# HGRN2's output gate by seven block products with weight sums made by DMA, in turn with a branch gate

## The chip, the cores and the metric

The kernel runs on one core of one Trainium2 chip. The metric is the device time of one execution in microseconds (us), as the median of several. The engines are named as in the profile: PE is TensorE (PEld its weight load), DVE is VectorE, ACT is ScalarE, POOL is GpSimd, and SP is SyncE, which here only issues DMAs.

## The reference

One decoder block on 256 tokens of width 1024 in fp32. Two token mixers read the same x by one input projection, are merged by gates, and a SwiGLU FFN follows.

```python
proj = einsum('bsd,dn->bsn', x, w_in)
hq, hf, hi, hg, mq, mk, mv, gates = split(proj)     # each 1024 wide, gates 2048
y = hgrn2_mixer(hq, hf, hi, lb)                     # the recurrence, 8 heads of 128
y = rms_norm(y, hgrn_norm_w) * silu(hg)             # norm per head; hg is the output gate
za = y @ w_branch_a                                 # branch a
zb = moba_attention(mq, mk, mv) @ w_branch_b        # branch b
ga, gb = split(sigmoid(gates + b_gate))             # the branch gates
x = layer_norm(ALPHA * x + (ga * za + gb * zb) @ w_out)
x = layer_norm(ALPHA * x + swiglu_ffn(x))
```

The step at issue is `hg = x @ w_in[:, 3072:4096]`, a product of 256x1024 by 1024x1024, and `silu(hg)`. Beside it are `gb`, a product of the same size, and the recurrence, whose work is done between the products.

## The kernel before

**Products.** TensorE multiplies numbers of a shorter format, so every fp32 operand is split into a high and a low half, and each product is made of three matmuls: high by high, low by high and high by low (`feat_steps`, lines 277 to 279; token-major in L296 to L298). x comes once, transposed, as xTr with its halves xTh and xTl. The weights come in tiles of 1 MB (128x2048 fp32), in the order of the list that `plan` makes. `stage` loads tile i into `raw` from SP's queue (pool `wraw`, three buffers), ACT casts it to the high half (`wh`, L195), DVE subtracts to get the low half (`wl`, L197); `wh` and `wl` have four buffers each, and `fetch` keeps the split three tiles ahead of TensorE (LOOKAHEAD = 3). A feature-major stage (hg, gb, ga, hq: `feat_pair`) takes four tiles of 256 columns with 48 matmuls of 128x256 each; a token-major one (hi: `tok_chunk`) has 128x512 matmuls.

**The order of the first 160 us** is that of the text: hf, hq, hi (tiles 8 to 11), hg (tiles 12 to 15), gb (16 to 19), ga (20 to 23), then the attention's mk, mq and mv. A scheduler then sets each engine's own row of instructions. Each engine works its row off in order, so an instruction that waits holds up all behind it.

**The recurrence** (`hgrn_steps`) is a generator that other stages advance by `side.step()`. It first makes Qt = Qg·Fg and kq = Kt·Qg with its halves kqh and kql, the diagonal products sd0 to sd3 on PE (L388, L389) and their masked copies into SD on DVE (L390). Then come seven levels (sc0 to sc6): two groups of matmuls (L404), masked copies into SD, and updates of Qt, Kt and Tt on DVE (L406 to L417). Then the state product sc7, the outputs o with their norm `on` (L445), and the transposes ot, in which `ya = pt * hgs` is split for branch a.

**The output gate**, before, is feature-major: Sigmoid on ACT, and DVE's `hgs = hg * norm weight * sigmoid(hg)` (L489). One level follows each hg, gb and ga tile.

**Banks.** PSUM has two pools of four banks: `mm` for the projections, `aux` for the recurrence. A product can begin when a bank of its pool has been read out; hi's four banks are freed by ACT's copies into hv (L481).

**The FFN's last part** (`quad`, q0 to q6) already uses seven products in place of eight for a 2x2 block product; the sums of its weight blocks are made by DVE (`mix`, table MIXES).

Of the kernel before, what the change touches and what calls it, by code (L numbers as in the profile page):

```python
# [10 lines left out]
F32 = mybir.dt.float32  # L11
# [6 lines left out]
P = 128  # L18
# [19 lines left out]
MIXES = (((0, 4, 0), 1, None), ((0, 4, 512), 0, 1), ((4, 4, 512), 0, 2), (None, 1, 2),  # L38
         (None, 2, None), ((4, 4, 0), 0, 3), (None, 3, None))
# [33 lines left out]
def plan():  # L73

    tiles = []

    def add(w, k0, kn, c0, n, held=False):
        tiles.append((w, k0, kn, c0 if isinstance(c0, tuple) else (c0,), n, held))
# [12 lines left out]
    feat("w_in", 0, 1024)  # L91
    tok("w_in", 2048, 1024)
    feat("w_in", 3072, 1024)
    feat("w_in", 8192, 1024)
    feat("w_in", 7168, 1024)
    for c in range(2):
        feat("w_in", 5120 + c * 512, 512)
        feat("w_in", 4096 + c * 512, 512)
        tok("w_in", 6144 + c * 512, 512)
    feat("w_branch_a", 0, 1024)  # L100
    feat("w_branch_b", 0, 1024)
    for k in range(0, KC, 2):
# [20 lines left out]
def hybrid_layer_kernel(ctx: ExitStack, tc, x, xT, vecs, wts, ln1_w, ln1_b, ln2_w, ln2_b, consts, out):  # L123
# [55 lines left out]
    def stage(pieces=None, eng=nc.vector):  # L179
        i = state["next"]  # L180
        if i >= len(loads):
            return
        state["next"] += 1
        _, _, k, _, _, held = loads[i]
        src = source(i).rearrange("p (k c) -> p k c", k=k)
        view = lambda z: z.rearrange("p (k c) -> p k c", k=k)
        raw = view(wraw.tile([P, 2048], F32, tag="raw", name=f"raw{i}"))
        if held:
            h, l = view(slot(f"wh{i}", F32R)), view(slot(f"wl{i}", F32R))
        else:  # L190
            h = view(whi.tile([P, 2048], F32R, tag="h", name=f"wh{i}"))
            l = view(wlo.tile([P, 2048], F32R, tag="l", name=f"wl{i}"))
        for ks in ks_of(pieces or (k,)):
            nc.sync.dma_start(raw[:, ks, :], src[:, ks, :])
            nc.scalar.copy(h[:, ks, :], raw[:, ks, :])  # L195
            yield
            eng.tensor_sub(l[:, ks, :], raw[:, ks, :], r32(h[:, ks, :]))  # L197
            yield
        ready.append((h, l))

    raws = []

    def mix():


        i = state["next"]
        state["next"] += 1
        tile, into, other = loads[i][-1]
        if tile is not None:
            kept = dict(pool=late, tag="late") if len(raws) < 2 else dict(pool=wraw, tag="raw")  # L210
            raws.append(kept.pop("pool").tile([P, 2048], F32, name=f"raw{i}", **kept))
            nc.sync.dma_start(raws[-1], source(i))
        into = len(raws) - 1 if tile is not None and other is None else into
        if other is not None:
            nc.vector.tensor_add(raws[into], raws[into], raws[other])  # L215
        h = whi.tile([P, 2048], F32R, tag="h", name=f"wh{i}")
        l = wlo.tile([P, 2048], F32R, tag="l", name=f"wl{i}")
        split(h, l, raws[into])
        view = lambda z: z.rearrange("p (k c) -> p k c", k=KW // 2)
        ready.append((view(h), view(l)))  # L220

    def fetch(ahead=LOOKAHEAD):
        while state["next"] < len(loads) and len(ready) < 1 + ahead:
            if isinstance(loads[state["next"]][-1], tuple):
                mix()
            else:
                list(stage())
        return ready.pop(0)
# [36 lines left out]
    def feat_pair(name, ah=None, al=None):  # L265
        ah, al = (xTh, xTl) if ah is None else (ah, al)
        wh, wl = fetch()
        ps = mm.tile([P, 2, T], F32, tag="mm", name=name)
        for f in range(2):
            feat_steps(ps[:, f, :], wh, wl, f, ah, al, range(KC))  # L270
        return ps

    def feat_steps(ps, wh, wl, f, ah, al, ks, k0=0):
        wcol = slice(f * P, (f + 1) * P)
        for k in ks:
# [3 lines left out]
            nc.tensor.matmul(ps, wl[:, k, wcol], ah[:, kk, :], start=False, stop=(kk == KC - 1))  # L279

# [68 lines left out]
    for j in range(4):  # L349
# [3 lines left out]
        for f in range(2):  # L353
            h = 2 * j + f
            nc.vector.scalar_tensor_tensor(Qg[:, :, h, :], by_half(ps[:, f, :]), lb[:, H + h:H + h + 1],
                                           by_half(sg[:, f, :]), op0=ALU.mult, op1=ALU.mult)
# [18 lines left out]
    def hgrn_steps():  # L375
        Qt, SD = halves(slot("Qt")), halves(slot("SD"))
        Tt = slot("Tt")
        nc.vector.tensor_mul(Qt, Qg, Fg)
# [13 lines left out]
        yield  # L392
        tot, size = Fg, NT * H * P
# [34 lines left out]
        on = slot("on").rearrange("p (t d) -> p t d", t=NT)  # L428
        for g in range(2):
            for u in range(NT):  # L430
# [14 lines left out]
                nc.vector.tensor_tensor(dst, ps, st[:, 8:12, None].to_broadcast([P, 4, P]), op=ALU.mult)  # L445
            yield
            for j in range(2):
# [27 lines left out]

    side = Steps()
# [3 lines left out]
    for c in range(2):  # L480
        for _ in tok_chunk(f"hi{c}", lambda t, ps: nc.scalar.copy(hv[:, t, c * 512:(c + 1) * 512], ps)):  # L481
            side.step()
    for j in range(4):
        ps = feat_pair(f"hg{j}")
        sg = hd2.tile([P, 2, T], F32, tag="sg", name=f"sgg{j}")
        nc.scalar.activation(sg, ps, AF.Sigmoid)
        for f in range(2):
            h = 2 * j + f
            nc.vector.scalar_tensor_tensor(hgs[:, h, :], ps[:, f, :], nw[:, h:h + 1], sg[:, f, :],  # L489
                                           op0=ALU.mult, op1=ALU.mult)  # L490
# [3 lines left out]
    def gates(name, b0):
        g = slot(name).rearrange("p (c t) -> p c t", c=KC)
        for j in range(4):
            ps = feat_pair(f"{name}{j}")
            for f in range(2):
                c = 2 * j + f
                nc.scalar.activation(g[:, c, :], ps[:, f, :], AF.Sigmoid, bias=bg[:, b0 + c:b0 + c + 1])  # L500
            side.step()
        return g
# [277 lines left out]
    def quad_product(n):  # L780
# [7 lines left out]
        for k in range(KW // 2):  # L788
            nc.tensor.matmul(ps, lh[:, k, :], wh[:, k, :], start=(k == 0), stop=False)
            nc.tensor.matmul(ps, lh[:, k, :], wl[:, k, :], start=False, stop=False)  # L790
            nc.tensor.matmul(ps, ll[:, k, :], wh[:, k, :], start=False, stop=(k == KW // 2 - 1))
# [19 lines left out]
    for j in range(EARLY, NF, 2):  # L811
        n = j // 2 % 2
        sums = []
        if j == KW:
            mixing = mixed_a()
        for i, (nm, p, tag) in enumerate([("g", mm, "mm"), ("u", aux, "aux")]):
# [8 lines left out]
            if j == KW:  # L825
                sh, sl = next(mixing)
# [59 lines left out]
```

## Time and profile before

| | |
|---|---|
| median of 3 runs | 508.87 us (508.49 to 509.5) |
| the profiled execution | 508.92 us, its span 506.9 us |
| mean granted TensorE clock | 0.995 of full |
| weight tiles | 78 DMAs of 1 MB by SP, median 4.8 us from issue to landing |
| bytes moved | 91.68 MB, of which 3.15 MB by POOL's queue (q0) |
| hi, hg, gb, ga (53.7 to 160 us) | PE busy 106.30 us of 106.30, DVE 89.25, ACT 51.13, POOL 4.02 |

Times in the rows of the profile are us from the span's start. A row of the timeline has the start, the duration, the engine, the line in the kernel, the operation, its output and inputs by the program's names, and in brackets how long the engine had been idle and what it waited for. A row of a group has, behind the bar, the busy time, the mean time of one in ns, and the idle time ahead of the group.

### The profile page before, as it was taken

Reading aid. Unit: us, or ns where it says so; the run is one execution under the profiler, and the core shown is the slowest. Engines: PE = TensorE matmul, PEld = TensorE weight load, DVE = VectorE, ACT = ScalarE, POOL = GpSimd, SP = SyncE. Lnnn points to the kernel's source line nnn. Section 1 sums busy time; section 2 is a strip of 40 time slices with the busy share of each in tenths; the row PEclk is TensorE's granted clock in tenths of the full one; section 3 lists DMA queues with packets and bytes.
Section 4 is the critical chain, followed back from the end, with each engine's and each line's share of the span. In section 5 each row is a group of like instructions: output and inputs, shape, how many; then the busy total and the mean of one; then the engine's idle time right before and its main releaser. Section 6 shows DMA issues by size and latency. Waiting matters only on the chain.

```text
span 506.9 us, 7897 instructions
## 1 busy us (share of the span) xinstructions
PE 496.7 (98%) x3308; PEld 457.9 (90%) x3308; DVE 363.8 (72%) x409; ACT 257.8 (51%) x312; POOL 39.9 (8%) x33
## 2 busy tenths in 40 slices
PE   8999999999999999999999999999999999999994
PEld 7999889999999998998999988888888888888884
DVE  4777799997565454676665599655687566989656
ACT  5795354354355554566544463354656655574500
POOL 0000000000020064263000000000000000000001
PEclk9999999999999999999999999999999999999998
DMA  7978444244423544544645776346545544154402
GB/s 236 393 280 319 180 170 164 93 162 162 166 85 140 194 167 173 182 163 149 250 180 185 277 272 210 123 166 215 200 167 180 220 181 166 36 213 178 154 1 83
DMA packets 15714, 91.68 MB, mean 181 GB/s; under 512 B 1856, under 2 KB 3008, under 8 KB 5696
## 3 DMA queue, kind: packets, MB, share of 16 engines
q1 hardware_dynamic: 14832, 88.04, 48.3%
q0 software_dynamic: 848, 3.15, 1.8%
q8 instruction: 26, 0.43, 0.3%
q14 instruction: 8, 0.07, 0.0%
HBM read 90.13 MB, written 1.05 MB: 180 GB/s over the span
## 4 chain that ended last, share of the span: by engine, by line
PE 94%; DMA 4%; DVE 1%; ACT 0%; SPq 0%; issue 0%; DVEq 0%
PE fu L748 7%; PE fg L748 7%; DMA raw<-in_wts_dram 4%; PE fg L749 3%; PE fu L749 3%; PE sc L404 3%; PE wd L612 3%; PE wd L610 3%; PE wd L611 3%; PE mk L279 2%; PE hq L279 2%; PE hq L278 2%; PE hq L277 2%; PE mk L278 2%; PE zb L279 2%; PE za L279 2%
## 5 line engine op out<-in xcount | busy, mean ns | idle before, releaser
L197 DVE TENSOR_TENSOR wl<-raw,wh 128x2048 fp32r<-128x2048 f32 (+2 forms) x84 | 177.4, 2114 | 92.5 <-ACT wh L195 92.2
L195 ACT CAST wh<-raw 128x2048 fp32r<-128x2048 f32 (+2 forms) x84 | 148.3, 1768 | 129.9 <-issue 14.1
L748 PE MATMUL fg<-x1p,wh 128*128 128x512 f32 x144 | 50.5, 394 | 0.0
L748 PE MATMUL fu<-x1p,wh 128*128 128x512 f32 x144 | 50.4, 394 | 0.0
L749 PE MATMUL fg<-x1p,wl 128*128 128x256 f32 x144 | 40.0, 278 | 0.0
L749 PE MATMUL fu<-x1p,wl 128*128 128x256 f32 x144 | 39.9, 277 | 0.0
L748 PEld LDWEIGHTS fu<-x1p,wh 128*128 128x128 f32 x144 | 27.0, 187 | 6.2
L748 PEld LDWEIGHTS fg<-x1p,wh 128*128 128x128 f32 x144 | 27.0, 187 | 6.1
L749 PEld LDWEIGHTS fg<-x1p,wl 128*128 128x128 f32 x144 | 27.0, 188 | 0.1
L749 PEld LDWEIGHTS fu<-x1p,wl 128*128 128x128 f32 x144 | 27.0, 188 | 0.0
L611 PE MATMUL wd<-wl,ah 128*128 128x512 f32 (+1 forms) x70 | 24.1, 347 | 0.0
L612 PE MATMUL wd<-wh,al 128*128 128x512 f32 (+1 forms) x70 | 24.1, 347 | 0.0
L610 PE MATMUL wd<-wh,ah 128*128 128x512 f32 (+1 forms) x70 | 23.7, 346 | 0.0
L279 PE MATMUL hf<-xTh,wl 128*128 128x256 f32 x64 | 18.6, 291 | 1.0 <-DVE wl L197 1.0
L277 PE MATMUL hf<-xTh,wh 128*128 128x256 f32 x64 | 18.2, 284 | 1.0 <-ACT wh L195 1.0
L279 PE MATMUL za<-yah,wl 128*128 128x256 f32 x64 | 18.5, 288 | 0.0
L278 PE MATMUL za<-yal,wh 128*128 128x256 f32 x64 | 18.4, 288 | 0.0
L277 PE MATMUL hg<-xTh,wh 128*128 128x256 f32 x64 | 18.4, 288 | 0.0
L172 ACT CAST wh<-raw 128x2048 fp32r<-128x2048 f32 x7 | 13.4, 1912 | 9.7 <-DVE raw L215 3.8
L173 DVE TENSOR_TENSOR wl<-raw,wh 128x2048 fp32r<-128x2048 f32 x7 | 16.0, 2287 | 3.2 <-ACT wh L172 3.2
L277 PE MATMUL mk<-xTh,wh 128*128 128x256 f32 x64 | 18.3, 286 | 0.0
L278 PE MATMUL mq<-xTl,wh 128*128 128x256 f32 x64 | 18.3, 286 | 0.0
(249 smaller groups left out, 1447.1 us busy)
## 6 DMA issues: line engine op xcount, KB each, us to landing
raw<-in_wts_dram SPq DMA_DIRECT2D x78, 1024.0 KB, 4.8
raw<-in_wts_dram SPq DMA_DIRECT2D x8, 256.0 KB, 5.0
xTr<-in_xT_dram SPq DMA_DIRECT2D x8, 128.0 KB, 4.9
raw<-in_wts_dram SPq DMA_DIRECT2D x2, 512.0 KB, 6.1
xr<-in_x_dram POOLq DMA_DIRECT2D x1, 1024.0 KB, 5.4
wb<-in_ln_w_dram POOLq DMA_DIRECT2D x2, 512.0 KB, 5.3
wb<-in_ln_b_dram POOLq DMA_DIRECT2D x2, 512.0 KB, 6.2
out_dram<-x SPq DMA_DIRECT2D x4, 256.0 KB, 2.0
```

What stands on the lines that cost most here:

```text
L173: nc.vector.tensor_sub(dst_l, src, r32(dst_h))
L195: nc.scalar.copy(h[:, ks, :], raw[:, ks, :])
L197: eng.tensor_sub(l[:, ks, :], raw[:, ks, :], r32(h[:, ks, :]))
L277: nc.tensor.matmul(ps, wh[:, k, wcol], ah[:, kk, :], start=(kk == 0), stop=False)
L278: nc.tensor.matmul(ps, wh[:, k, wcol], al[:, kk, :], start=False, stop=False)
L279: nc.tensor.matmul(ps, wl[:, k, wcol], ah[:, kk, :], start=False, stop=(kk == KC - 1))
L404: nc.tensor.matmul(ps[:, a, :], KL[:, h, :], later(Qt, n, h, 1), start=True, stop=True)
L610: nc.tensor.matmul(ps, lh(kk)[:, ts], wh[:, k, ns], start=(kk == base), stop=False)
L611: nc.tensor.matmul(ps, lh(kk)[:, ts], wl[:, k, ns], start=False, stop=False)
L612: nc.tensor.matmul(ps, ll(kk)[:, ts], wh[:, k, ns], start=False, stop=(kk == ktot - 1))
L748: nc.tensor.matmul(ps, wh[:, k, wcol], x1p.both(k), start=(k == 0), stop=False)
L749: nc.tensor.matmul(ps[:, 0, :], wl[:, k, wcol], x1p[0, k, slice(0, T)], start=False, stop=(k == KC - 1))
```

## The change

The output gate becomes token-major, and its product is made of seven block products (`quad_stage`, `block_product`) of 12 matmuls of 128x512 each, in place of 192 matmuls of 128x256. The tokens are two blocks of 128, the inputs two of 512, the columns two of 512. Four of the products multiply sums of weight blocks (s and t, three states of s) by differences of activations (`differences`: xs, with halves xSh and xSl, made during hq).

The sums are made in the `raw` buffers: four blocks are loaded by SP as before, and then POOL issues DMAs that add a block from DRAM onto a buffer (`accum_op`). The table BY_DMA has, for each product, the buffer that it uses and what is done ahead of it: s = block 11; s += block 12; t = block 12 and t += block 22; s += 22; v = 21; u = 22; s += 21. Every state of s is split (ACT, DVE) before the next sum may overwrite it.

```diff
+BY_DMA = (("s", (("load", "s", 11),)), ("s", (("onto", "s", 12),)), ("t", (("load", "t", 12), ("onto", "t", 22))),
+          ("s", (("onto", "s", 22),)), ("v", (("load", "v", 21),)), ("u", (("load", "u", 22),)),
+          ("s", (("onto", "s", 21),)))
+GATES_BEHIND = (0, 2, 4, 5)
...
-    feat("w_in", 3072, 1024)
-    feat("w_in", 8192, 1024)
+    for n, recipe in enumerate(BY_DMA):
+        mix("hg", "w_in", 0, 3072, recipe)
+        if n in GATES_BEHIND:
+            feat("w_in", 8192 + 256 * GATES_BEHIND.index(n), 256)
...
+            if op == "load":
+                own, tag = (late, "late") if name == "wd" and dst in "st" else (wraw, "raw")
+                raws[key] = own.tile([P, 2048], F32, tag=tag, name=f"raw{i}{dst}")
+                nc.sync.dma_start(raws[key], wts[src])
+            elif op == "onto":
+                nc.gpsimd.dma_start(raws[key], wts[src], accum_op=ALU.add)
...
+    def block_product(ps, lh, ll, wh, wl, first=True, last=True):
+        for k in range(KW // 2):
+            go = dict(skip_group_check=not (first and last))
+            nc.tensor.matmul(ps, lh[:, k, :], wh[:, k, :], start=first and k == 0, stop=False, **go)
+            nc.tensor.matmul(ps, lh[:, k, :], wl[:, k, :], start=False, stop=False, **go)
+            nc.tensor.matmul(ps, ll[:, k, :], wh[:, k, :], start=False, stop=k == KW // 2 - 1, **go)
...
+        if j == 0:
+            xs = slot("xs")[:, 0:1024].rearrange("p (i k t) -> p i k t", i=2, k=KW // 2)
+            xSh, xSl = mixed4(slot("xSh", F32R)), mixed4(slot("xSl", F32R))
+            mixing = differences(lambda t, k: xTr[:, k:k + 4, t * P:(t + 1) * P], xs, xSh, xSl)
+        if j in (1, 2):
+            next(mixing)
...
-        kq, kqh, kql = slot("kq"), slot("kqh", F32R), slot("kql", F32R)
+        kq, kqh, kql = flat(Qg), slot("kqh", F32R), slot("kql", F32R)
...
+                row = on[:, u, g * 512:(g + 1) * 512]
+                nc.vector.tensor_mul(row, row, hgs[:, u, g * 512:(g + 1) * 512])
...
-                ya = hd2.tile([P, 2, T], F32, tag="sg", name=f"ya{g}{j}")
-                nc.vector.tensor_mul(ya, pt, hgs[:, h0:h0 + 2, :])
-                split(yah[:, h0:h0 + 2, :], yal[:, h0:h0 + 2, :], ya)
+                for a in range(2):
+                    h = h0 + a
+                    nc.scalar.activation(yah[0][:, h, :], pt[:, a, :], AF.Copy, scale=nw[:, h:h + 1])
+                    nc.vector.scalar_tensor_tensor(yal[0][:, h, :], pt[:, a, :], nw[:, h:h + 1], r32(yah[0][:, h, :]),
+                                                   op0=ALU.mult, op1=ALU.subtract)
...
-        sg = hd2.tile([P, 2, T], F32, tag="sg", name=f"sgg{j}")
-        nc.scalar.activation(sg, ps, AF.Sigmoid)
-        for f in range(2):
-            h = 2 * j + f
-            nc.vector.scalar_tensor_tensor(hgs[:, h, :], ps[:, f, :], nw[:, h:h + 1], sg[:, f, :],
-                                           op0=ALU.mult, op1=ALU.mult)
-        side.step()
...
-    gb = gates("gb", KC)
-    ga = gates("ga", 0)
+    def gate_pair(g, name, b0, j, p=mm):
+        ps = feat_pair(f"{name}{j}", p=p)
+        for f in range(2):
+            c = 2 * j + f
+            nc.scalar.activation(g[:, c, :], ps[:, f, :], AF.Sigmoid, bias=bg[:, b0 + c:b0 + c + 1])
+    gb = slot("gb").rearrange("p (c t) -> p c t", c=KC)
+    hg = quad_stage("hg", xTh, xTl, xSh, xSl, hgs, lambda z, src: nc.scalar.activation(z, src, AF.Silu))
+    for j in range(4):
+        next(hg)
+        gate_pair(gb, "gb", KC, j, aux)
+        if j >= 1:
+            side.step()
+    list(hg)
+    ga = slot("ga").rearrange("p (c t) -> p c t", c=KC)
+    for j in range(4):
+        gate_pair(ga, "ga", 0, j)
+        side.step(2)
```

`quad_stage` makes the products in the banks b[0] to b[3] of `mm`, and combines them with one ACT copy each of b[0] and b[2], six DVE sums or differences of 128x512, and ACT's Silu. The FFN's `quad` does the same work as before by the shared functions. The tiles are now numbered 12 (s), 13 (gb0), 14 (s), 15 (t), 16 (gb1), 17 (s), 18 (v), 19 (gb2), 20 (u), 21 (gb3), 22 (s), and 23 to 26 for ga. The gates gb are written into banks of `aux`.

The first place is VectorE's row at the end of hi and the beginning of hg. Names have the tile's number: wl12 is the low half of tile 12, raw12s the buffer of s. Before:

```order
L378 TENSOR_TENSOR Qt_677<-Qg_96,Fg_94 128x2048
L381 TENSOR_TENSOR kq_681<-Kt_95,Qg_96 128x2048
L197 TENSOR_TENSOR wl12_754<-raw12_752,wh12_753 128x2048
L414 TENSOR_TENSOR Kt_95<-Kt_95,Fg_94 128x512x2
L383 TENSOR_TENSOR kql_683<-kq_681,kqh_682 128x2048
L197 TENSOR_TENSOR wl13_805<-raw13_803,wh13_804 128x2048
L197 TENSOR_TENSOR wl14_852<-raw14_850,wh14_851 128x2048
L390 TENSOR_TENSOR SD_678<-sd0_687,ident_89 128x512
```

And now the same place:

```order
L419 TENSOR_TENSOR Qt_685<-Qg_96,Fg_94 128x2048
L188 TENSOR_TENSOR wl12_744<-raw12s_741,wh12_743 128x2048
L422 TENSOR_TENSOR Qg_96<-Kt_95,Qg_96 128x2048
L212 TENSOR_TENSOR wl13_777<-raw13_775,wh13_776 128x2048
L456 TENSOR_TENSOR Kt_95<-Kt_95,Fg_94 128x512x2
L424 TENSOR_TENSOR kql_689<-Qg_96,kqh_688 128x2048
L188 TENSOR_TENSOR wl14_807<-raw12s_741,wh14_806 128x2048
L431 TENSOR_TENSOR SD_686<-sd0_693,ident_89 128x512
```

In both, the low half of tile 14 stands ahead of SD's product with sd0; tile 14 was a plain load, and is now the second state of s, in the buffer that tile 12 was split from.

The second place is TensorE's row at the end of hi. Before:

```order
L296 MATMUL hi1_1_802<-wh11_706,xTh_86 128x512
L389 MATMUL sd0_687<-kql_683,ones_91 128x512
L389 MATMUL sd1_691<-kql_683,ones_91 128x512
L389 MATMUL sd2_695<-kql_683,ones_91 128x512
L389 MATMUL sd3_699<-kql_683,ones_91 128x512
L297 MATMUL hi1_1_802<-wh11_706,xTl_87 128x512
```

Eleven more matmuls of hi follow there, and then hg0. Now:

```order
L337 MATMUL hi1_1_774<-wl11_713,xTh_86 128x512
L430 MATMUL sd0_693<-kql_689,ones_91 128x512
L430 MATMUL sd1_697<-kql_689,ones_91 128x512
L430 MATMUL sd2_701<-kql_689,ones_91 128x512
L430 MATMUL sd3_705<-kql_689,ones_91 128x512
L295 MATMUL gb0_869<-xTh_86,wh13_776 128x256
```

The sd products now stand behind all of hi, and gate gb0, which takes its bank from the same pool as sd0 to sd3, follows them directly; hg0 stands 29 matmuls later.

The third place is the row of POOL's queue, which had no DMA between the program's start and the attention. Now:

```order
L941 UNCONDITIONAL_BRANCH
L231 DMA raw15t_843<-in_wts_dram 128x2048
L231 DMA raw12s_741<-in_wts_dram 128x2048 x3
L487 ISA
L487 TENSOR_TENSOR ost00_1522<-ost00_1522,half_92 128x4
```

The accumulate onto t stands first, ahead of the three onto s.

More of the change, by code (lines that the diff above doesn't have):

```diff
@@ L37 @@
 KW = 8
-MIXES = (((0, 4, 0), 1, None), ((0, 4, 512), 0, 1), ((4, 4, 512), 0, 2), (None, 1, 2),
-         (None, 2, None), ((4, 4, 0), 0, 3), (None, 3, None))
+BY_SUMS = (("s", (("load", "s", 11),)), ("s", (("load", "t", 12), ("sum", "s", "t"))),
+           ("s", (("load", "u", 22), ("sum", "s", "u"))), ("t", (("sum", "t", "u"),)), ("u", ()),
+           ("s", (("load", "v", 21), ("sum", "s", "v"))), ("v", ()))
+BY_DMA = (("s", (("load", "s", 11),)), ("s", (("onto", "s", 12),)), ("t", (("load", "t", 12), ("onto", "t", 22))),
+          ("s", (("onto", "s", 22),)), ("v", (("load", "v", 21),)), ("u", (("load", "u", 22),)),
+          ("s", (("onto", "s", 21),)))
+GATES_BEHIND = (0, 2, 4, 5)
 ORDER_DOWN = (0, 1, "t", 2, "t", 3, "t", 4, "t", 5, 6) + ("t",) * HOLD_DOWN
@@ L73, in plan, with block, mix @@
 def plan():
-    tiles = []
-    def add(w, k0, kn, c0, n, held=False):
-        tiles.append((w, k0, kn, c0 if isinstance(c0, tuple) else (c0,), n, held))
+    blocks, steps = [], []
+    def block(*key):
+        if key not in blocks:
+            blocks.append(key)
+        return blocks.index(key)
+    def add(w, k0, kn, c0, n, held=False):
+        steps.append((block(w, k0, kn, c0 if isinstance(c0, tuple) else (c0,), n), kn, held, None))
+    def mix(name, w, k0, c0, recipe):
+        at = {10 * i + j: (w, k0 + (i - 1) * KW // 2, KW // 2, (c0 + (j - 1) * 512,), 512)
+              for i in (1, 2) for j in (1, 2)}
+        into, ops = recipe
+        ops = [(op, dst, src if op == "sum" else block(*at[src])) for op, dst, src in ops]
+        steps.append((None, KW // 2, False, (name, into, ops)))
     def feat(w, c0, n):
@@ L114, in plan @@
             k += 2
-        elif MIXES[step][0] is not None:
-            add("w_ffn_down", *MIXES[step][0], 512, MIXES[step])
-        else:
-            tiles.append((None, 0, 0, (0,), 0, MIXES[step]))
-    return tiles
+        else:
+            mix("wd", "w_ffn_down", 0, 0, BY_SUMS[step])
+    return blocks, steps
 @with_exitstack
@@ L162, in both @@
             return self.parts[i][:, k, :, :]
-    loads = plan()
+    loads = plan()[1]
     ready = []
     state = {"next": 0}
-    stored = np.cumsum([w[0] is not None for w in loads]) - 1
-    source = lambda i: wts[int(stored[i])]
     def split(dst_h, dst_l, src):
@@ L183, in stage @@
         state["next"] += 1
-        _, _, k, _, _, held = loads[i]
-        src = source(i).rearrange("p (k c) -> p k c", k=k)
+        at, k, held, _ = loads[i]
+        src = wts[at].rearrange("p (k c) -> p k c", k=k)
         view = lambda z: z.rearrange("p (k c) -> p k c", k=k)
@@ L207, in mix @@
         state["next"] += 1
[L208 to L215, printed above, removed]
+        name, into, ops = loads[i][-1]
+        for op, dst, src in ops:
+            key = name, dst
+            if op == "load":
[4 more added lines that the diff above has]
+                nc.gpsimd.dma_start(raws[key], wts[src], accum_op=ALU.add)
+            else:
+                nc.vector.tensor_add(raws[key], raws[key], raws[name, src])
         h = whi.tile([P, 2048], F32R, tag="h", name=f"wh{i}")
         l = wlo.tile([P, 2048], F32R, tag="l", name=f"wl{i}")
-        split(h, l, raws[into])
+        split(h, l, raws[name, into])
         view = lambda z: z.rearrange("p (k c) -> p k c", k=KW // 2)
@@ L223, in fetch @@
         while state["next"] < len(loads) and len(ready) < 1 + ahead:
-            if isinstance(loads[state["next"]][-1], tuple):
+            if loads[state["next"]][-1] is not None:
                 mix()
@@ L262, in lower_bounds, with feat_pair @@
         nc.vector.tensor_scalar(lb[:, H:2 * H], lb[:, 0:H], -1.0, 1.0, op0=ALU.mult, op1=ALU.add)
-    def feat_pair(name, ah=None, al=None):
+    def feat_pair(name, ah=None, al=None, p=mm):
         ah, al = (xTh, xTl) if ah is None else (ah, al)
         wh, wl = fetch()
-        ps = mm.tile([P, 2, T], F32, tag="mm", name=name)
+        ps = p.tile([P, 2, T], F32, tag="mm" if p is mm else "aux", name=name)
         for f in range(2):
@@ L279, in feat_steps, with differences @@
             nc.tensor.matmul(ps, wl[:, k, wcol], ah[:, kk, :], start=False, stop=(kk == KC - 1))
+    def block_product(ps, lh, ll, wh, wl, first=True, last=True):
[4 more added lines that the diff above has]
+            nc.tensor.matmul(ps, ll[:, k, :], wh[:, k, :], start=False, stop=k == KW // 2 - 1, **go)
+    def differences(a, s, h, l):
+        for i, (n, m) in enumerate(((a(1, 0), a(1, 4)), (a(0, 0), a(1, 0)))):
+            nc.vector.tensor_sub(s[:, i], n, m)
+        split(h[:, 0:2], l[:, 0:2], s)
+        yield
+        nc.vector.tensor_sub(s[:, 0], a(0, 0), s[:, 0])
+        nc.vector.tensor_sub(s[:, 1], a(0, 4), s[:, 0])
+        split(h[:, 2:4], l[:, 2:4], s)
+        yield
+    mixed4 = lambda z: z.rearrange("p (i k t) -> p i k t", i=4, k=KW // 2)
     def feat_first(pss, tiles):
@@ L474, in drain @@
                 self.step()
+    yah, yal = [], []
     side = Steps()
@@ L481, in hybrid_layer_kernel, with quad_stage @@
         for _ in tok_chunk(f"hi{c}", lambda t, ps: nc.scalar.copy(hv[:, t, c * 512:(c + 1) * 512], ps)):
+            pass
+    hgs = slot("hgs").rearrange("p (t d) -> p t d", t=NT)
+    lo, hi = slice(0, 512), slice(512, D)
+    def quad_stage(name, ah, al, sh, sl, dst, final):
+        plain = lambda t, k: (ah[:, k:k + KW // 2, t * P:(t + 1) * P], al[:, k:k + KW // 2, t * P:(t + 1) * P])
+        mixed = lambda i: (sh[:, i], sl[:, i])
+        b = [mm.tile([P, 512], F32, tag="mm", name=f"{name}{i}") for i in range(4)]
+        p = hd2.tile([P, 512], F32, tag="sg", name=f"{name}p")
+        block_product(b[0], *plain(0, 0), *fetch())
+        nc.scalar.copy(p, b[0])
+        yield
+        block_product(b[1], *mixed(0), *fetch())
+        nc.vector.tensor_sub(dst[:, 0, hi], b[1], p)
+        block_product(b[2], *mixed(1), *fetch())
+        nc.scalar.copy(dst[:, 1, hi], b[2])
+        yield
+        block_product(b[3], *mixed(2), *fetch())
+        nc.vector.tensor_sub(dst[:, 1, lo], p, b[3])
+        nc.vector.tensor_sub(dst[:, 1, hi], b[3], dst[:, 1, hi])
+        block_product(b[0], *plain(0, 4), *fetch(), first=False)
+        final(dst[:, 0, lo], b[0])
+        nc.vector.tensor_add(dst[:, 1, hi], dst[:, 1, hi], dst[:, 0, hi])
+        final(dst[:, 1, hi], dst[:, 1, hi])
+        yield
+        block_product(b[3], *mixed(3), *fetch(), first=False)
+        nc.vector.tensor_add(dst[:, 0, hi], dst[:, 0, hi], b[3])
+        final(dst[:, 0, hi], dst[:, 0, hi])
+        yield
+        block_product(b[2], *plain(1, 4), *fetch(), first=False)
+        nc.vector.tensor_add(dst[:, 1, lo], dst[:, 1, lo], b[2])
+        final(dst[:, 1, lo], dst[:, 1, lo])
@@ L494, in gates @@
[L494 to L502, printed above, removed]
-    gb = gates("gb", KC)
-    ga = gates("ga", 0)
+        gate_pair(ga, "ga", 0, j)
+        side.step(2)
     side.drain()
@@ L787, in quad_product @@
         ps = mm.tile([P, 512], F32, tag="mm", name=f"q{n}")
[L788 to L791, printed above, removed]
+        block_product(ps, lh, ll, wh, wl)
         p, f = kept[:, 0, :], kept[:, 1, :]
@@ L814, in hybrid_layer_kernel @@
         if j == KW:
-            mixing = mixed_a()
+            sh, sl = mixed4(slot("sh", F32R)), mixed4(slot("sl", F32R))
+            mixing = differences(lambda t, k: araw[:, k:k + 4, t * P:(t + 1) * P],
+                                 kept.rearrange("p i (k t) -> p i k t", k=KW // 2), sh, sl)
         for i, (nm, p, tag) in enumerate([("g", mm, "mm"), ("u", aux, "aux")]):
@@ L825, in hybrid_layer_kernel @@
             if j == KW:
-                sh, sl = next(mixing)
+                next(mixing)
         i, k = divmod(j, KC)
@@ L870 @@
         .reshape(kn, P, -1).transpose(1, 0, 2).reshape(P, -1)
-        for w, k0, kn, c0, n, _ in plan() if w is not None])
+        for w, k0, kn, c0, n in plan()[0]])
     nc = _bacc.Bacc("TRN2", target_bir_lowering=False, num_devices=1)
```

27 lines of the change are left out of this document (6 added, 21 removed).

## The prediction

> **What bounds the kernel now.** I read the engines' busy shares first, then the chain of work that ended last, then TensorE's waits, then the busy time by stretches around the change.
>
> ```profile
> PE 496.7 (98%) x3308; PEld 457.9 (90%) x3308; DVE 363.8 (72%) x409; ACT 257.8 (51%) x312; POOL 39.9 (8%) x33
> PE 94%; DMA 4%; DVE 1%; ACT 0%; SPq 0%; issue 0%; DVEq 0%
> ```
>
> TensorE (PE) is busy 98% of the span and makes up 94% of the chain: each matmul taken away is worth its whole time, as long as PE goes on finding its operands, and each new wait of PE is paid in full. The waits say how little it waits today, and the stretches show the place:
>
> ```profile
> engine line waited for: us in total, times, longest us
> PE warm L324 <- DVE half L325: 1.1, 1, 1.1
> PE hf L277 <- ACT wh L195: 1.0, 1, 1.0
> ...
> core 0: us, PE busy (x) PEld busy (x) DVE busy (x) ACT busy (x) POOL busy (x), PEclk, DMA share, GB/s
> 53.70:77.20 23.50, 23.50 (x105) 19.40 (x104) 21.48 (x15) 11.46 (x9) 0.00 (x0) 1.00 0.54 200
> 77.20:108.40 31.20, 31.20 (x258) 31.18 (x257) 30.88 (x32) 13.94 (x12) 0.00 (x0) 1.00 0.37 132
> 108.40:134.00 25.60, 25.60 (x219) 25.60 (x219) 19.79 (x19) 12.42 (x13) 0.00 (x0) 1.00 0.42 149
> 134.00:160.00 26.00, 26.00 (x225) 26.00 (x224) 17.11 (x23) 13.32 (x19) 4.02 (x4) 1.00 0.34 122
> ```
>
> The four stretches are the value projection hi, then hg, gb and ga. PE is busy in all 106.3 us of them at full clock (1.00), so nothing but its own work can be saved there. VectorE (DVE) is the second engine: 30.88 of 31.20 us in the hg stretch, where it makes the weights' low halves and runs the recurrence's levels. POOL does nothing before 134 us, and the DMA engines are busy 34 to 54%.
>
> **What it saves on PE.** A pitch is read from start to start over many matmuls.
>
> ```profile
> 77.22 0.28 PE L277 MATMUL hg<-xTh,wh 128*128 128x256 f32 x1
> 81.04 0.28 PE L278 MATMUL hg<-xTl,wh 128*128 128x256 f32 x1
> 86.78 0.28 PE L278 MATMUL hg<-xTl,wh 128*128 128x256 f32 x1
> 441.86 0.39 PE L789 MATMUL q<-wh,ah 128*128 128x512 f32 x1
> 447.33 0.39 PE L610 MATMUL wd<-wh,ah 128*128 128x512 f32 x1
> ```
>
> Between 81.04 and 86.78 lie 48 matmuls of 256 columns: 0.1196 us each. Between 441.86 and 447.33 lie two block products of the FFN, 24 matmuls of 512 columns, the form that hg gets: 0.228 us each. Before: 4 tiles x 48 = 192 x 0.1196 = 22.96 us. After: 7 products x 12 = 84 x 0.228 = 19.14 us. The saving is 3.8 us; it can't be more, since PE loses nothing else here.
>
> **What it adds beside PE.** The price rows:
>
> ```profile
> L197 DVE TENSOR_TENSOR wl<-raw,wh 128x2048 fp32r<-128x2048 f32 x15 | 34.5, 2297 | 11.1 <-ACT wh L195 11.0
> L489 DVE SCALAR_TENSOR_TENSOR hgs<-hg,vec,sgg 128x256 f32<-128x256 f32 x8 | 3.4, 468 | 0.0
> L445 DVE TENSOR_TENSOR on<-o,ost 128x512 f32<-128x512 f32 x4 | 2.8, 692 | 3.6 <-POOL ost L443 3.6
> L390 DVE TENSOR_TENSOR SD<-sd,ident 128x512 f32<-128x512 f32 x4 | 2.6, 684 | 0.0
> ```
>
> ```profile
> 55.59 2.29 DVE L197 TENSOR_TENSOR wl<-raw,wh 128x2048 fp32r<-128x2048 f32 x1 [2.69 <-ACT wh L195]
> ...
> 94.80 1.21 DVE L414 TENSOR_TENSOR Kt<-Kt,Tt 128x1024 f32<-128x1024 f32 x1
> ```
>
> Seven tiles are split where four were: 3 x 2.30 = 6.9 us. The blocks' sums are 6 operations of 128x512 (0.69, as SD) for the eight scalings of 0.47: +0.4. The product with the gate is 4 x 0.69 = 2.8, and the norm's weight moves into the low half, about +0.8. DVE gets some 11 us more in stretches where it was busy 89.25 of 106.3: 100 of the 102.5 left. It fits, but only because the levels start later, in gb1, and o moves into mk and mq, where DVE has room (19.79 of 25.60 and 17.11 of 26.00 in the stretches ahead). The activations' differences in the hq stage cost DVE 4 x 0.69 and two low halves 1024 wide of 1.21, 5.2 us; they lie in its idle time there, of which the gap ahead of tile 11's low half is one (2.69, the row at 55.59). ACT is busy half the time. I cost all of these at nothing; the cover is DVE's slack, and a rival below is that it runs out.
>
> **What it adds on the path: the accumulating DMAs.** The first one into s, for the second product, is awaited thus. Tile 14's high half (ACT) waits for it; tile 14's low half stands in DVE's row ahead of SD's product with sd0; that product frees the bank into which gate gb0, PE's next work after hi, is written. Behind tile 14 on ACT stand tile 15's cast and the hv copies that free hg0's banks. So PE's first gb0 matmul waits for a DMA whose product comes some 9 us later. Before, the same place held no DMA that had to follow other work. The rows for the chain:
>
> ```profile
> 57.80 0.87 DVE L355 SCALAR_TENSOR_TENSOR Qg<-hq,lb,sgq 128x256 f32<-128x256 f32 x2
> 58.70 2.29 DVE L378 TENSOR_TENSOR Qt<-Qg,Fg 128x2048 f32<-128x2048 f32 x1
> 59.01 1.92 ACT L195 CAST wh<-raw 128x2048 fp32r<-128x2048 f32 x1 [2.96 <-PE hi L297]
> raw<-in_wts_dram SPq DMA_DIRECT2D x78, 1024.0 KB, 4.8
> xr<-in_x_dram POOLq DMA_DIRECT2D x1, 1024.0 KB, 5.4
> wb<-in_ln_b_dram POOLq DMA_DIRECT2D x2, 512.0 KB, 6.2
> GB/s 393 208 11 0 66 339 437 415 153 0 0 87 131 339 393 437 11 0 0 0 0 87 131 339 437 404 22 0 0 0 87 218 426 448 371 448 426 371 0 0
> ```
>
> The last row is the DMA rate from 50 to 80 us in slices of 0.75 us. A load streams at up to 437 GB/s: 1.049 MB in 2.4 us. The plain 1 MB load from POOL lands after 5.4, so 3.0 of it is fixed.
>
> Step by step: tile 11's low half ends at 55.59 + 2.29 = 57.9. That frees t's buffer; its load lands 4.8 later, at 62.7, and POOL issues t's accumulate, which stands first in POOL's queue, so the one for s can't go before. DVE goes on with Qg 0.87, the differences' low half (1024 wide, 1.21), Qt 2.29 and tile 12's low half 2.29: 64.5. Then s may be overwritten, and its accumulate is issued. Call E the time it lands. After E come the cast 1.92, the low half 2.29 and SD 0.69: gb0 can begin at E + 4.9. PE is through with hi and sd at 77.2, as before. **The stall is E + 4.9 - 77.2 = E - 72.3**, and not below the 0.2 us or so that gb0 waits for sd0's own product, which stood half under hi before.
>
> No row shows an accumulate. Lower end: it streams like a plain POOL load. Then t lands at 62.7 + 5.4 = 68.1 and s 2.4 behind it at 70.5: no stall. Upper end: the slowest POOL row, wb, with 0.5 MB in 6.2 - 3.0 = 3.2, or 6.4 per MB: t 72.1, s 78.5, and with the plain load of tile 16, which begins near 70 and shares the same DMA engines, 2.4 more, 80.9: a stall of 8.6. I take 4.8 per MB, near the middle of 2.4 and 6.4, because an accumulate has two streams of 1 MB to fetch, the weights and the sum that stands in SBUF, and 4.8 is two plain streams. Then t lands at 62.7 + 3.0 + 4.8 = 70.5, s at 75.3 behind it, up to 77.7 with all of tile 16's share; I take 76. The stall is 3.7.
>
> The Trainium skill, "Collectives: The Full Stack", section "The bandwidth ceiling: the fold count and why AG ≠ RS ≠ AR", says that an adding transfer needs two source reads on one read ring and so runs at about half a copy's rate, measured 1.93. By that the stream would take 2.4 x 1.93 = 4.6 per MB (an estimate from that page), s would land 0.4 earlier than my sum has it, and the stall be some 3.3; no run here shows it yet.
>
> The two later accumulates into s wait for tiles 14 and 17, and their products come some 20 and more us later, so even at 6.4 per MB they land in time. The DMA bytes rise by 4 MB (8 loads where 4 were); in the coarse shares above there is room. SP's queue holds its loads in order, and t's load waits at 57.9 for a buffer as tile 14's did before.
>
> **The sum.** -3.8 (matmuls) + 3.7 (gb0's wait) + 0 (the rest, covered) = -0.1. The profiled execution took 508.92, 2.0 outside its span of 506.9; the median of the runs is 508.87, the same within 0.05. So 508.8. About 0.2% (1.0 us) is what a measurement of this kernel can tell from no change.
>
> **Rivals.**
> - *The accumulates are hidden* (plain rate, or the two at once): E below 72.5, only 0.2 us of waiting. -3.8 + 0.2 = -3.6: 505.3. For it: the DMA share of 0.54 in the hi stretch, and POOL's empty queue. Against it: a second stream must be read, and s is queued behind t.
> - *Slow accumulates*: from E of about 77.1 on, the kernel is slower by over 0.2%, since the stall then passes 4.8. By the wb rate the stall is 8.6: -3.8 + 8.6 = +4.8, 513.7. For it: wb's 6.2 us for half the bytes on POOL's queue. Against it: xr's 5.4 for a whole MB on the same queue.
> - *The clock drops.* Before, PE never waited over 1.1 us and its clock stands at 1.00 in all four stretches. With a stall of 3.7 it stops for longer than this profile ever shows. If gb0's first 29 matmuls (29 x 0.12 = 3.5 us) ran at half rate, that would add 3.5: 512.3. The Trainium skill, "TensorE: Matmul & The Clock Gate", "Part 1: The HAM clock gate (the "warmup" mystery)", gives half rate after an idle window of about 3.4 us, until as long a stretch of work; by that rule the likeliest case stands just at the edge, and no wait here is long enough to test it.
> - *DVE runs out.* It idles while tile 14 and later tile 17 wait for their sums, and has 100 of 102.5 us to fill. By the order of its row, the low halves for gb3 and hg5 stand behind the whole first level, and I find only about 0.6 us there. If DVE is 4 us late, 512.8.
>
> **Chances.** Accumulates at about two streams (E 73.5 to 77.7, net -2.6 to +1.6): 0.44, of which 0.10 faster, 0.23 within 0.2%, 0.11 slower. Hidden: 0.25, faster. Slow accumulates: 0.19; the clock 0.06; DVE 0.06: slower. So faster 0.35, same 0.23, slower 0.42. The range reaches from the hidden case, 505.0, to the slow one, 514.0; the likeliest case alone is 506.3 to 510.5.
>
> **What would show it.** In the changed kernel's profile: 84 hg matmuls 128x512 at a pitch of 0.228 for the saving; PE's waits, where gb0 or hg0 should wait some 3.7 us near 77 us for DVE's SD or ACT's hv; the landing of POOL's loads into s and t, 5.4 us if plain, 7 to 11 by my price; the granted clock between 77 and 90, and DVE's idle time ahead of tile 14. The prediction is wrong if PE doesn't stop at gb0, or if its largest wait stands elsewhere, at hg5 or gb3.

## The result: slower, and the profile after

The changed kernel takes 515.6 us (515.2 to 515.92), the one before 509.12 in the same comparison: a ratio of 1.0128, with an interval of 1.0111 to 1.0146. The forecast was 508.8, its range 505.0 to 514.0. The sign that held the largest chance came out; the time lies 1.6 above the range. Ratios here are of fast executions alone: one of the kernel before (614.26) and one of the kernel with plain loads (543.62), both at a lower granted clock throughout, are left out of them.

TensorE's waits, the first table to read, have one new row:

```profile
engine line waited for: us in total, times, longest us
PE gb L295 <- DVE SD L431: 7.0, 1, 7.0
```

It is the place that the prediction named, gb0 behind SD, but 7.0 us and not 3.7. Stretches around it show the second loss (columns as before: busy time of each engine, granted clock, DMA share, GB/s):

```profile
77.90:80.20 2.30, 0.00 (x0) 0.00 (x0) 0.00 (x0) 0.16 (x1) 0.00 (x0) 1.00 0.43 175
80.20:84.92 4.72, 0.00 (x1) 0.01 (x1) 2.95 (x3) 4.72 (x5) 0.36 (x1) 0.51 0.00 0
84.92:90.40 5.48, 5.48 (x25) 5.48 (x26) 3.93 (x4) 0.76 (x2) 0.49 (x1) 0.50 0.83 145
90.40:94.00 3.60, 3.60 (x21) 3.11 (x20) 0.00 (x0) 0.12 (x1) 0.00 (x0) 0.99 0.96 328
```

The granted clock falls to half 2.3 us into the wait and stays there for 5.5 us after work has begun again. The timeline shows the wait, in brackets, and further down two rows of the same form (gb, L295) at two speeds, 0.41 and 0.28 us:

```profile
84.92 0.58 PE L295 MATMUL gb<-xTh,wh 128*128 128x256 f32 x1 [7.03 <-DVE SD L431]
85.29 0.42 PE L296 MATMUL gb<-xTl,wh 128*128 128x256 f32 x1
...
90.21 0.41 PE L295 MATMUL gb<-xTh,wh 128*128 128x256 f32 x1
...
93.80 0.28 PE L295 MATMUL gb<-xTh,wh 128*128 128x256 f32 x1
```

From 85.29 to 90.21 are 23 matmuls at 0.214 us, where 0.1196 was the pitch; 26 matmuls start before the clock is back, and cost 26 x 0.094 = 2.4 us.

What was waited for, followed backwards, on VectorE, ScalarE, POOL's queue and by the DMA issues of the first two accumulates (KB each, us to landing):

```profile
81.97 2.29 DVE L188 TENSOR_TENSOR wl<-raw12s,wh 128x2048 fp32r<-128x2048 f32 x1 [8.47 <-ACT wh L187]
84.18 2.48 DVE L431 TENSOR_TENSOR SD<-sd,ident 128x512 f32<-128x512 f32 x4
...
80.04 1.90 ACT L187 CAST wh<-raw12s 128x2048 fp32r<-128x2048 f32 x1 [11.16 <-DMA raw12s<-in_wts_dram]
...
63.90 1.05 POOL L231 DMA_DIRECT2D raw15t<-in_wts_dram  x1 [63.45 <-DMA raw15t<-in_wts_dram]
65.04 0.86 POOL L231 DMA_DIRECT2D raw12s<-in_wts_dram  x1
...
raw12s<-in_wts_dram POOLq DMA_DIRECT2D x1, 1024.0 KB, 14.9
raw15t<-in_wts_dram POOLq DMA_DIRECT2D x1, 1024.0 KB, 9.6
raw<-in_wts_dram SPq DMA_DIRECT2D x1, 1024.0 KB, 11.0
```

The sum into s is issued at 65.0 and lands 14.9 later, at 80.0; t's, ahead of it, needs 9.6, and tile 16's plain load, issued at 69.3 beside them, 11.0. Then come cast, low half and SD, as the prediction's chain has them: 80.0 + 1.9 + 2.3 + 0.7 = 84.9.

The busy share of the DMA engines (in tenths) and what they moved, from 55 to 85 us in slices of 0.75 us, show the adding itself:

```profile
DMA  9930058799000093999899999799997800000000
GB/s 404 448 131 0 0 87 120 328 426 415 22 0 0 0 175 66 218 218 240 175 229 208 218 218 306 186 240 284 306 295 273 339 22 0 0 0 0 0 0 0
```

At a share of 9 the plain load near 61.5 us (t's first block) moves 415 to 426 GB/s; from 67 to 73 us, with the sums, the engines are as busy (8 to 9) and move 175 to 240, about half. They have work until 79 us.

The account closes to 0.3 us. In the timeline, the last matmul of hf starts at 30.4 before and 30.9 after, the last of wd at 499.5 and 505.9. Between them are 469.1 and 475.0 us, 5.9 more: -3.8 (fewer matmuls) + 7.0 (wait) + 2.4 (clock) = 5.6. The other 0.3 isn't traced; the kernel with plain loads, below, has as much. The rest of the span's 6.8 lies in hf, whose last matmul starts anywhere from 30.3 to 31.9 in the ten profiles of this case, and in the tail.

### The profile page after: what moved, and what is told of

The parts are those of the page before. It is cut to its first block, busy times and chain, and to the rows that moved or that the text cites. A ratio compares the mean times of both kernels' runs of the same rounds, so it can differ in the third digit from the quotient of the medians.

```text
span 513.7 us, 7724 instructions
## 1 busy us (share of the span) xinstructions
PE 496.1 (97%) x3200; PEld 453.1 (88%) x3200; DVE 377.4 (73%) x420; ACT 275.5 (54%) x329; POOL 44.3 (9%) x37
## 4 chain that ended last, share of the span: by engine, by line
PE 82%; DVE 1%; DVEq 0%; issue 0%
PE fu L826 6%; PE fg L826 6%; PE fg L827 3%; PE fu L827 3%; PE sc L446 3%; PE wd L690 3%; PE wd L689 3%; PE wd L688 2%; PE gb L295 2%; PE gb L297 2%; PE gb L296 2%; PE zb L296 1%; PE zb L297 1%; PE mq L295 1%; PE mk L297 1%; PE ga L297 1%
## 5 line engine op out<-in xcount | busy, mean ns | idle before, releaser
L212 DVE TENSOR_TENSOR wl<-raw,wh 128x2048 fp32r<-128x2048 f32 (+2 forms) x80 | 168.5, 2108 | 77.3 <-ACT wh L210 76.8
L210 ACT CAST wh<-raw 128x2048 fp32r<-128x2048 f32 (+2 forms) x80 | 140.8, 1762 | 97.5 <-PE fg L826 12.6
L295 PE MATMUL gb<-xTh,wh 128*128 128x256 f32 x64 | 19.4, 304 | 7.0 <-DVE SD L431 7.0
L295 PEld LDWEIGHTS gb<-xTh,wh 128*128 128x128 f32 x64 | 13.5, 210 | 7.6 <-DVE SD L431 7.5
L297 PE MATMUL gb<-xTh,wl 128*128 128x256 f32 x64 | 19.3, 301 | 0.0
L296 PE MATMUL gb<-xTl,wh 128*128 128x256 f32 x64 | 19.2, 300 | 0.0
L295 PE MATMUL hf<-xTh,wh 128*128 128x256 f32 x64 | 18.3, 286 | 0.9 <-ACT wh L210 0.9
L295 PE MATMUL mq<-xTh,wh 128*128 128x256 f32 x64 | 18.4, 287 | 0.0
```

What stands on the lines that cost most here:

```text
L295: nc.tensor.matmul(ps, wh[:, k, wcol], ah[:, kk, :], start=(kk == 0), stop=False)
L296: nc.tensor.matmul(ps, wh[:, k, wcol], al[:, kk, :], start=False, stop=False)
```

## The experiments

The theory: the loss is one wait, made by a row order in which gb0 hangs on the accumulate into s, and by the clock that falls in that wait; nothing else of the change costs anything that shows. The rivals: the adding isn't what is slow; VectorE has too much to do; the slow matmuls have another cause. Below, a ratio is to the kernel before in the same comparison (509.38 in the first four, 509.37 in the last four).

**Plain loads in place of the adding ones** (the sums are left out).

```diff
-                nc.gpsimd.dma_start(raws[key], wts[src], accum_op=ALU.add)
+                nc.gpsimd.dma_start(raws[key], wts[src])
```

> The changed kernel with the four accumulating DMAs made plain loads on the same queue, in the same order and rows (the sums are left out). Theory (the adding itself halves the stream): each of the two streams 1 MB in 2.4 us, so t lands near 69.5 and s near 72; gb0 waits less than 1 us and the clock stays up: 505.5. Rival (POOL's queue, its descriptors or sharing with tile 16's load is what is slow, not the adding): s lands at 77 or later and the time stays above 511.

Measured: 505.8, ratio 0.9938 (0.9923 to 0.9952). TensorE has no new wait. The same three transfers, in the same order, now take:

```profile
raw15t<-in_wts_dram POOLq DMA_DIRECT2D x1, 1024.0 KB, 5.2
raw12s<-in_wts_dram POOLq DMA_DIRECT2D x1, 1024.0 KB, 7.8
raw<-in_wts_dram SPq DMA_DIRECT2D x1, 1024.0 KB, 6.0
```

5.2, 7.8 and 6.0 for 9.6, 14.9 and 11.0. So the adding is what is slow, and all else that the change adds (splits, the other sums, differences, late levels, 4 MB more) is covered: from hf's end to wd's the profile has 465.6 us, 3.5 less than before, of the 3.8 that the matmuls save.

**The diagonal products four times over**, to keep TensorE at work during the wait.

```diff
-            nc.tensor.matmul(row, ones, kqh[:, cs], start=True, stop=False)
-            nc.tensor.matmul(row, ones, kql[:, cs], start=False, stop=True)
+            for _ in range(4):
+                nc.tensor.matmul(row, ones, kqh[:, cs], start=True, stop=False)
+                nc.tensor.matmul(row, ones, kql[:, cs], start=False, stop=True)
```

> The changed kernel with the diagonal products sd0 to sd3 computed four times over into the same banks, 24 more matmuls of 128x512 (5.5 us) in the time in which TensorE waited for the accumulate. Theory (2.4 us of the loss are the clock that fell during the wait): gb0 still begins near 84.9, after a wait of about 1.5, the clock stays at 1.00, its first 26 matmuls take 0.12 instead of 0.21: 513.2, 2.4 less than the changed kernel. Rival (the slow matmuls have another cause, such as the DMAs that run there): the pitch stays 0.21 and the time 515.6 or more.

Measured: 512.33, ratio 1.0059 (1.0047 to 1.0071), 3.3 less than the changed kernel, with 24 matmuls more.

```profile
77.90:83.50 5.60, 5.60 (x26) 4.38 (x24) 1.23 (x1) 3.17 (x2) 0.00 (x0) 1.00 0.19 73
83.50:84.57 1.07, 0.16 (x1) 0.00 (x0) 1.07 (x2) 1.07 (x3) 0.00 (x0) 1.00 0.00 0
84.57:94.00 9.43, 9.43 (x64) 8.80 (x65) 6.88 (x6) 3.99 (x6) 0.85 (x1) 1.00 0.78 195
```

The clock stays at 1.00, and with it the pitch, beside DMAs at 195 GB/s: the 2.4 us are the clock's. Of the other 0.9, 0.35 is that the scheduler now put hg0 ahead of gb0, and hg0 starts at 84.57 where gb0 had started at 84.92; the rest is within what executions differ by.

**SD ahead of tile 14's low half on VectorE.** `behind` adds an edge of order alone between instructions of one engine; no wait is taken away. `ahead_of["dve"]` holds SD's four products.

```diff
-        split(h, l, raws[name, into])
+        if i == 14:
+            high = nc.scalar.copy(h, raws[name, into])
+            low = nc.vector.tensor_sub(l, raws[name, into], r32(h))
+            behind(low, ahead_of["dve"])
+        else:
+            split(h, l, raws[name, into])
```

> The changed kernel with the first edge alone: SD's four products ahead of tile 14's low half; hv's copies still stand behind the casts of tiles 14 and 15 on ScalarE. Theory: gb0 begins at about 78.1 and its first 29 matmuls end at 81.6; hg0 waits for hv's first copy, that is E (80.0) + 2 x 1.9 + 0.5 = 84.3, a wait of 2.7; the clock may just stay up: 508 to 510.5. Rival (only SD's place mattered, ScalarE is never late): 505.4, as with both edges.

Measured: 510.43, ratio 1.0027 (1.0014 to 1.0039). gb0 starts at 77.9, as expected, and hg0 waits for hv:

```profile
PE hg L314 <- ACT hv L543: 2.6, 1, 2.6
...
81.60:84.20 2.60, 0.05 (x1) 0.00 (x0) 2.29 (x2) 2.60 (x4) 0.00 (x0) 1.00 0.00 0
84.20:85.70 1.50, 1.50 (x6) 1.26 (x7) 1.50 (x1) 1.42 (x3) 0.85 (x1) 0.96 0.00 0
85.70:88.90 3.20, 3.20 (x10) 2.54 (x9) 0.70 (x1) 0.32 (x1) 0.00 (x0) 0.50 0.97 156
```

A wait of 2.6 us was enough to lower the clock, and it fell only 1.5 us after the wait had ended, for 3.2 us: another 1.6 lost. The mean clock is 0.990 to 0.994 in all seven executions of this kernel, and 0.995 to 0.998 in all twelve of the next, which takes this wait away.

**And hv's copies ahead of tile 14's high half on ScalarE.** `ahead_of["act"]` holds hv's four copies; so that they are written ahead of tile 14, the last fetch of hi looks two tiles ahead and not three.

```diff
             behind(low, ahead_of["dve"])
+            behind(high, ahead_of["act"])
...
-            wh, wl = fetch()
+            wh, wl = fetch(2 if name == "hi1" and q else LOOKAHEAD)
```

> The changed kernel with two edges in the order of work: SD's four products stand ahead of tile 14's low half on VectorE, and hv's four copies ahead of tile 14's high half on ScalarE. Nothing else is changed. Theory (the row order hangs gb0 on the accumulate, and nothing else is lost): the accumulate into s still lands near 80 us, but gb0 begins at about 78.1, TensorE never waits over 1 us, the clock stays at 1.00, and the saving of 3.8 comes through: 505.4, ratio to before 0.993. Rival 1 (VectorE is short of time as well): waits of some us appear at gb3 or hg5 instead, 507 to 512. Rival 2 (the accumulate is waited for whatever the order): hg1, which needs tile 14, stalls by 2 us or more, 507.5 or above.

Measured: 509.16, ratio 0.9998 (0.9989 to 1.0007): no gain over before. The theory's 505.4 missed; the time lies in the range of its first rival, a VectorE short of time, which the waits bear out for one of two:

```profile
PE sc L460 <- ACT kl L455: 1.6, 1, 1.6
PE hg L316 <- DVE wl L188: 1.6, 1, 1.6
```

TensorE no longer stops at gb0 or hg0, and the clock stays up, but it waits 1.6 us for tile 20's low half near 115 us and, near 142 us, 1.6 for a copy of kl (an operand that ScalarE copies for each level). The first stands behind a VectorE that had idled ahead of the sums and is then busy without a gap, 8.00 of 8.00 us in the two stretches around it:

```profile
83.06 2.29 DVE L245 TENSOR_TENSOR wl<-raw12s,wh 128x2048 fp32r<-128x2048 f32 x1 [2.34 <-ACT wh L244]
...
96.39 2.29 DVE L188 TENSOR_TENSOR wl<-raw12s,wh 128x2048 fp32r<-128x2048 f32 x1 [4.40 <-ACT wh L187]
...
108.00:116.00 8.00, 6.63 (x55) 6.31 (x53) 8.00 (x7) 5.72 (x5) 0.00 (x0) 1.00 0.39 164
116.00:124.00 8.00, 7.77 (x54) 7.32 (x55) 8.00 (x7) 7.38 (x8) 0.00 (x0) 1.00 0.83 303
```

So the late sums cost twice: at gb0, and, if that is mended, later by VectorE's lost time. (With plain loads it had enough.)

The second wait ends with ScalarE. TensorE is free at 141.3; VectorE's Qt for that level is done at 142.1, ScalarE's copy of kl at 142.8, though the Kt that it copies had been done at 136.7. In between ScalarE works off a Silu, a cast, a table load of 1.28 us and a gate's Sigmoid. The change adds six such loads (ten where four were): in ScalarE's row one stands at each turn from Sigmoid to Silu and back.

**t's sum left out** (t is block 12 alone).

```diff
-BY_DMA = (("s", (("load", "s", 11),)), ("s", (("onto", "s", 12),)), ("t", (("load", "t", 12), ("onto", "t", 22))),
+BY_DMA = (("s", (("load", "s", 11),)), ("s", (("onto", "s", 12),)), ("t", (("load", "t", 12),)),
```

> The changed kernel without t's accumulating DMA (t is block 12 alone, its sum is left out); every other row is in the same order. Theory (the accumulate into s was late mostly because t's stood ahead of it in the same queue): s is issued near 64.6 and lands after 3.0 + 4.8, at 72.5, or 75 with all of tile 16's load beside it; gb0 waits 0.2 to 2.5 us instead of 7.0: 506 to 508.5. Rival (s is slow by itself): it lands at 78 or later and gb0 waits over 5 us with a lower clock, 512 or above.

Measured: 507.1, ratio 0.9953 (0.994 to 0.9966). The wait at gb0 is down to

```profile
PE gb L295 <- DVE SD L431: 1.4, 1, 1.4
```

s was issued at 64.46 and its cast starts at 73.78, 9.3 later in place of 15.0. Most of what made s late was t's accumulate ahead of it.

**t's accumulate behind s's, all sums made.** `sums` holds the accumulating DMAs as they are written, s's first.

```diff
-                nc.gpsimd.dma_start(raws[key], wts[src], accum_op=ALU.add)
+                sums.append(nc.gpsimd.dma_start(raws[key], wts[src], accum_op=ALU.add))
+                if i == 15:
+                    behind(sums[1], sums[:1])
```

> The changed kernel with one edit: t's accumulating DMA stands behind the first one of s on POOL's queue, so it's issued about 1 us later and after it. All sums are made. Theory (the queue serves them in order): s lands at 72.5 to 75, gb0 waits 0.2 to 2.5 us, t lands near 80, in time for its product near 90: 506 to 508.5. Rival (both share the DMA engines at once, whatever the order): s still lands near 79, gb0 waits 6 us or more and the clock falls: 513 to 515.6.

Measured: 508.48, ratio 0.9982 (0.9973 to 0.9991): 7 us faster than the changed kernel by exchanging two DMAs that are issued a microsecond apart. The sum issued first lands first:

```profile
64.81 1.05 POOL L239 DMA_DIRECT2D raw12s<-in_wts_dram  x1 [64.36 <-DVE wl L188]
65.53 1.23 POOL L239 DMA_DIRECT2D raw15t<-in_wts_dram  x1
...
74.78 1.91 ACT L187 CAST wh<-raw12s 128x2048 fp32r<-128x2048 f32 x1 [6.14 <-DMA raw12s<-in_wts_dram]
...
PE gb L305 <- DVE SD L441: 2.0, 1, 2.0
PE hg L312 <- ACT hv L540: 0.6, 1, 0.6
```

s's cast starts at 74.8 and not 80.0, t lands 15.9 after its issue, in time for its product. Two waits are left, 2.6 us together, with 3.7 us of work between them, and the clock stays at 1.00 in the profiled execution. (Two of the eleven executions have a mean clock of 0.993, as the kernel with a wait of 2.6 had; whether it fell there isn't shown.)

**All three edits of order**: s's accumulate first, SD and hv ahead of tile 14, by the diffs above.

> Three edits of order together: s's accumulate ahead of t's on POOL's queue, SD's products ahead of tile 14's low half on VectorE, hv's copies ahead of tile 14's high half on ScalarE. Theory (with both edits of SD and hv alone, 509.2, the rest of the loss is 1.6 us at tile 20's low half and 1.6 at a copy of kl, both behind a VectorE that had idled for the accumulates): s's states come 5 us earlier, VectorE idles that much less, both waits go: 505.5. Rival (VectorE has too much to do in any case): the two waits stay within half a us each, 508 to 509.

Measured: 506.19, ratio 0.9935 (0.9922 to 0.9949), faster than both kernels. TensorE's only new wait is

```profile
PE sc L463 <- ACT kl L458: 0.6, 1, 0.6
```

From hf's end to wd's are 466.1 us, 3.0 less than before: -3.8 + 0.6, and 0.2 untraced. The wait for tile 20's low half is gone, as the theory had it; that for kl's copy is shorter, and again a table load (at 135.4) stands ahead of the copy (137.4).

**And Tt's products ahead of tile 17's low half**, which `ahead_of["s3"]` holds, for the Tt of every level.

```diff
-                nc.vector.tensor_mul(nxt, free_view(tot, 0, [[2, size // 2]]), free_view(tot, 1, [[2, size // 2]]))
+                tt = nc.vector.tensor_mul(nxt, free_view(tot, 0, [[2, size // 2]]), free_view(tot, 1, [[2, size // 2]]))
+                if True:
+                    behind(ahead_of["s3"], [tt])
```

> As the kernel with three edits of order, and in addition the products Tt of all levels (1.2 + 0.7 + 0.4 + three of 0.2, some 3 us, which need only Fg) stand ahead of tile 17's low half, in the time in which VectorE would wait for its sum. Theory: where tile 17's sum still comes late, 1.8 us of VectorE's idle time are filled: 505.3, as good as or better than the kernel with three edits by up to 1. Rival (nothing waits there any more): no difference from it.

Measured: 507.13, ratio 0.9946 (0.9933 to 0.9959), no better than the kernel with three edits (the intervals overlap); from hf's end to wd's it has the same 466.1 us, and kl's wait of 0.6 is still there. TensorE waits for nothing there any more, and VectorE's idle time ahead of tile 17 was only 1.4 us in the kernel with three edits: nothing to gain, as the rival said.

## Why the prediction was wrong, point by point

- *The saving*, -3.8: right. Of it, 3.5 came through in the kernel with plain loads and 3.0 in the one with three edits of order.
- *The cover* of what DVE and ACT get, cost at nothing: right as long as the sums are early (plain loads: no new wait). Where they are late and gb0 no longer waits for them, VectorE runs out at tile 20, the product called hg5, as that rival had it: 1.6 us late. With early sums the margin there is 1.2 us (in the kernel with three edits the low half ends at 111.8 and is first used at 113.0); the forecast's 0.6 isn't measured. For ScalarE the forecast left the six table loads out. Their 7.7 us fit in, but the copy of kl that TensorE waits for stands behind one; no run takes them away.
- *The chain* E + 4.9 - 77.2: right. With the E of the trace, 80.0, it gives 7.7; PE was through at 77.9, so 7.0.
- *The price of an accumulate*, two plain streams: right for the rate, and at the low end of what landings showed. A later one, with a plain load beside it, took

```profile
raw12s<-in_wts_dram POOLq DMA_DIRECT2D x1, 1024.0 KB, 7.9
```

 which is the 3.0 + 4.8 of the prediction. Less the fixed 3.0, it is 4.9 where a plain load has 2.4, a ratio of 2.0. Over all kernels of this case, though, the second and third sums into s took 7.8 to 9.3, and the first sum on the queue 9.2 to 9.9. The Trainium skill ("Collectives: The Full Stack", "The bandwidth ceiling: the fold count and why AG ≠ RS ≠ AR") says of ReduceScatter that its add needs two source reads, and gives 1.93 between copy and add; this row's 2.0 is near it.
- *The landing time*, "s at 75.3 behind it ... I take 76": this is the step that failed, by 4.0, for s landed at 80.0. By the rows, t was issued at 63.9 for 62.7 (+1.2, of which 0.5 a general lag of that execution), it took 9.6 for 7.8 (+1.8), and s landed 6.5 behind it for 4.8 (+1.7); 0.7 of these 4.7 the forecast had allowed for tile 16's load. What the DMA engines moved from 64 to 74 us (queue, packets, MB, share of the engines' time; q0 is POOL's queue, q1 SP's) tells more:

```profile
q0 software_dynamic: 210, 1.59, 83.9%
q1 hardware_dynamic: 16, 0.13, 3.3%
```

 t landed at 73.5. By 74 us the two sums had moved 1.59 MB, all of t and 0.54 of s, and tile 16's load only 0.13. The rest of s (0.51 MB) and the rest of tile 16 (0.92) were still to move, and landed together, at 80.0 and 80.3. I had put 0.7 of tile 16's 2.4 ahead of s's end, and nearly all of it was. The three streams together, 4.8 + 4.8 + 2.4 = 12.0 us from 63.9 + 3.0, would have ended at 78.9. Open is the other 1.1, and why the first sum on the queue needs 9.2 even where t's is left out; nor does a run take tile 16's load away, so its part is worked out and not tested. The wait was thus sized at 3.7 in place of 7.0.
- *The clock* is the second step that failed: it stood as a rival of its own, 0.06, with a price of 3.5, and at nothing in the sum. It isn't a rival: it follows from the wait, and the wait that I forecast, 3.7, lies between the 2.6 and the 7.0 that both brought it. It cost 2.4. Wait and clock together, -3.8 + 7.0 + 2.4 = 5.6, give 514.5 and leave the range, whose upper end had the longer wait but not the clock behind it.
- *Slow accumulates* ended at 513.7, with s at 80.9 and a wait of 8.6, close to what came, but for the wrong reason: it had 6.4 per MB for t and s in a row and all of tile 16's load behind that, where the sums ran at about half a plain load's rate and shared the engines.

## What to carry to other kernels

A transfer on the critical path is priced with everything that streams beside it: list all DMAs in flight between its issue and its landing and add their streams; here the one that was waited for landed with the last. Where two slow transfers are issued close together, put the one that is waited for first; here that order alone was worth 7 us. A wait of a TensorE that has run without a stop is to be priced with the clock behind it: here 2.6 us brought it, and 2.0 us in the profiled execution didn't. Where two functions alternate on ScalarE, count the table loads too, here 1.28 us each.

## What the runs showed of the hardware

The clock's fall isn't tied to the end of the wait. After a wait of 7.0 us it had fallen 2.3 us into it and came back 5.5 us after work began; after one of 2.6 us it fell 1.5 us after work had begun and came back 3.2 us later; waits of 1.4 and 2.0 us left it alone in their profiled executions. The Trainium skill, "TensorE: Matmul & The Clock Gate", "What's actually happening", gives half rate after an idle window of about 3.4 us, and says that the window runs freely. The half rate agrees; that a wait of 2.6 us suffices, and that the clock falls 2.3 us into a longer one, doesn't agree with a window of 3.4 us that must be wholly idle, and here the measurement decides. The wait then costs a second time, 1.6 to 2.4 us, where the prediction had priced it at 3.5.
